# Regrouping modulation steps, moving key transposes in the emitted order, and moving small latent-attention operations between engines, in a two-layer trunk on one core

## The chip, the cores and the metric

The kernel runs on one core of one Trainium2 chip. The metric is the time of one launch in device microseconds (us). The engines are called PE (TensorE, matmuls and transposes), PEld (its loads of stationary operands), DVE (VectorE), ACT (ScalarE), POOL (GpSimd) and SP (SyncE, which issues the DMAs here). Each engine works through its own queue in order and waits at an instruction until the semaphores say that its inputs and its output buffer are ready.

## The reference, cut to what matters

One inference step of a trunk with two layers. 128 prompt tokens and 1024 latent tokens of width 1024 run through each. Layer 0 holds grouped-query attention with rotary keys and a pooling mixer; layer 1 holds a neighbourhood attention (C) and a multi-head latent attention (D) over 128 cached, 1024 latent and 128 prompt keys. Both layers are modulated by shift, scale and gate rows that come from a matmul of the conditioning vector with `w_mod`.

```python
def adaln(cond, w, b):                       # w: 1024 x 3072, cond: the latent request and the prompt
    m = (silu(cond) @ w + b)[:, None, :]
    return split_last(m, (D_MODEL, D_MODEL, D_MODEL))     # shift, scale, gate
def pre_norm(x, g, mod):
    return rms_norm(x, g) * (1 + mod[1]) + mod[0]
def post_residual(x, y, g, mod):
    return x + mod[2] * rms_norm(y, g)
# layer 0, mixer A
q, k, v, ga, ub, gb = split_last(h @ w_in, EVEN_IN_SIZES)  # 512, 128, 128, 512, 512, 512
q, k = axial_rope(rms_norm(q, q_norm)), axial_rope(rms_norm(k, k_norm))
o_a = softmax(q k^T) v ; y = concat(o_a * silu(ga), o_b * silu(gb)) @ w_out
# layer 1, mixer D (8 heads, 64 + 32 columns each)
qd = (rms_norm(cq, q_norm) @ w_uq)                         # w_uq: 384 x 768
kv = (ckv_all @ w_ukv)                                     # w_ukv: 256 x 1024
k_d = concat(kv[..., :64], kpe_all for every head)
o_d = softmax(q_d k_d^T) v_d
```

Everything is float32.

## The kernel before, in words

**Arithmetic.** A float32 product is made of three matmuls in the type fp32r: high times high, high times low and low times high part (`mm3`). So each operand is split into two parts: the high part is a cast, the low part a subtraction. The helpers that record an operation have one line each, and by these lines the profile names them: L97 a matmul, L106 a transpose on TensorE, L109 a DMA on SP's queue, L113 `acopy` (a copy or cast on ScalarE), L118 `vcopy` (the same on VectorE), L121 `vtt` (two tensors on VectorE), L124 `ptt` (two tensors on POOL), L131 `vts` (tensor and scalar on VectorE). L947 is the reduction of the row maxima on VectorE, L952 prepares the maxima for a matmul, L979 is the exponential, L1976 the fill value in `kstep`.

**Order.** No scheduler orders the work: it is emitted by hand, engine by engine in that order. Two functions do the mixing. `weave(main, fill, frac)` (L31) emits a main list of (cost, step) pairs and puts the steps of a fill list between them in proportion to their costs; a step `None` in a fill list emits nothing and only takes up cost. `merge(a, b, off)` (L46) emits the first `off` steps of one fill list and then mixes in another.

**Buffers.** Two pools of slabs hold most operands: "s" (25 buffers) and "w" (17 buffers). PSUM has two tags, A with three banks and B with five (`kn.B` and `kn.C` both take from B). A bank or slab is handed out in the order of the program; the first instruction that writes to it waits for the last one that used it before.

**Stages** (times of the profiled execution): key and value projection of layer 0 to about 70 us; its q stage 70 to 142; gates and the pooling mixer to about 320; the attention units of layer 0 to about 545; the output projection; projections and neighbourhood attention of layer 1 from about 656 to 1090; the token phase of the latent attention to about 1165; its units to about 1500; the last output projection to the end.

**Modulation.** Rows are made by matmuls whose stationary operand is 32 columns wide (`self.sil(k)`, the tile silrep) and which fill one of four 32-row groups of a PSUM bank each. `mod_ss(l)` makes the shift and scale rows: per step k of eight, four matmuls of 512 columns, with two weight slabs wm loaded one step ahead. `mod_gate(l)` makes the gate rows: per k, four matmuls of 256 columns with one slab wg. The layer-1 shift and scale rows are fill steps of the q stage, the gate rows of layer 0 fill steps of items 8 and 9 of the gate stage (on "w" slabs), those of layer 1 fill steps of the first attention unit of layer 0 (on "s" slabs).

**The q stage.** `q_main(0)` and `q_main(1)` are the two halves (256 columns of q each). Each half fills five banks "qkv" with two token tiles each (the fifth holds one), and after each bank `q_evac` norms, scales and rotates the queries (VectorE and ScalarE, rotary partly on POOL). The fill steps of the first half are the keys: `kv1` (norm), `kv2` (rotary on POOL), `kv3` (transposes kT on TensorE, then the casts KH on ScalarE and the subtractions KL on VectorE), and `wl.need(1)`, the split of the second weight chunk.

**The latent attention.** `load_uk`/`split_uk` and `load_uq`/`split_uq` load and split the weights of the next pair of heads (two units); `kstep` makes the keys of a column range in the tile dK, and for the prompt keys (column 1152) in a small tile dKQ, which also takes the rotary key part kpp and a row of ones. The row maxima run ahead of the exponentials: pieces of score matmuls mp are reduced on VectorE (L947), their prepared negatives ms are turned by matmuls mT into a row that is added in the score matmuls st; the exponentials P feed pv, and on POOL the sums acc.

## Time and profile before

| | |
|---|---|
| median of three runs | 1620.8 us (1619.03, 1620.8, 1624.38) |
| profiled execution, its own time | 1616.9 us |
| its span | 1615.1 us |
| mean granted TensorE clock | 0.975 |
| TensorE matmuls busy | 1532.7 us (95%) |
| stationary loads | 1244.7 us (77%) |
| VectorE | 814.4 us (50%) |
| ScalarE | 646.7 us (40%) |
| POOL | 612.7 us (38%) |
| DMA | 104.81 MB, 65 GB/s on the mean |

A profiled row is read like this: start in us, length, engine, line, operation, output and inputs by their tile names, then the shape, the number of instructions, and in brackets the wait ahead of it in us with the instruction that ended it. A row of waits gives the waiting and the releasing instruction, and then the waits' sum, their number and the longest. A row of stretches gives start and end, length, the busy time of PE, PEld, DVE, ACT and POOL with the number of instructions, the granted clock (1.00 is full speed), the busy share of the DMA engines and GB/s.

### The profile page before, as it was taken

How to read it: one execution, taken by the hardware profiler on the slowest of the kernel's cores; microseconds unless marked ns; L12 is line 12 of the kernel's file. 1: busy time of each engine (PE TensorE's matmuls, PEld its weight loads, DVE VectorE, ACT ScalarE, POOL GpSimd, SP SyncE). 2: the span in 40 equal slices, each digit the busy share in tenths (PEclk: the TensorE clock that was granted, in tenths of full speed). 3: DMA queues.
4: the chain of work that ended last, by engine and by line, in shares of the span. 5: the costliest groups of instructions: out<-in, count | busy, mean ns of one | idle time of the engine just before them, and what ended most of it. 6: DMA issues, size and time to landing. Idle time of an engine off the chain costs nothing.

```text
span 1615.1 us, 23601 instructions
## 1 busy us (share of the span) xinstructions
PE 1532.7 (95%) x9095; PEld 1244.7 (77%) x9095; DVE 814.4 (50%) x1796; ACT 646.7 (40%) x1371; POOL 612.7 (38%) x487
## 2 busy tenths in 40 slices
PE   7989999989899999899999999999999899999998
PEld 5978998945555588898989898999966566565786
DVE  4565232347575645534344444424665665645633
ACT  5332211255555333444444544443444343444311
POOL 2643212058669324541303113001156554556421
PEclk8999999999999999999999999999999999999999
DMA  9253004120001122410504131040000000013341
GB/s 345 85 199 86 27 27 150 53 86 14 1 14 40 65 105 79 94 30 15 97 16 82 30 75 38 21 145 11 11 8 20 15 26 15 20 41 104 108 145 52
DMA packets 114080, 104.81 MB, mean 65 GB/s; under 512 B 41776, under 2 KB 99952, under 8 KB 113968
## 3 DMA queue, kind: packets, MB, share of 16 engines
q1 hardware_dynamic: 113792, 103.23, 21.4%
q8 instruction: 72, 1.18, 0.3%
q14 instruction: 40, 0.33, 0.1%
q10 hardware_dynamic: 176, 0.07, 0.0%
HBM read 87.54 MB, written 15.75 MB: 64 GB/s over the span
## 4 chain that ended last, share of the span: by engine, by line
PE 79%; DVE 10%; ACT 5%; issue 3%; POOL 2%; DMA 1%; DVEq 0%; ACTq 0%; SPq 0%; POOLq 0%
PE cg L97 15%; PE yps L97 11%; PE st L97 8%; PE gate L97 8%; PE pv L97 8%; PE lat L97 4%; PE mp L97 4%; PE cpv L97 3%; PE cS L97 2%; PE cT L106 2%; PE dq L97 2%; DVE mx L947 2%; PE qkv L97 2%; PE kv L97 1%; PE modps L97 1%
## 5 line engine op out<-in xcount | busy, mean ns | idle before, releaser
L947 DVE TENSOR_REDUCE mx<-mp 128x1 f32<-128x384 f32 x384 | 189.9, 547 | 108.7 <-PE mp L97 107.3
L124 POOL TENSOR_TENSOR acc<-acc,P 128x1024 f32<-128x1024 f32 x84 | 201.1, 2394 | 86.3 <-ACT P L979 82.5
L979 ACT ACTIVATE P<-st 128x512 f32<-128x512 f32 x256 | 148.1, 598 | 159.1 <-PE st L97 149.3
L124 POOL TENSOR_TENSOR wlo<-raw,whi 128x1024 fp32r<-128x1024 f32 x36 | 87.3, 2427 | 266.9 <-ACT whi L113 205.3
L97 PE MATMUL yps<-whi,ohl 128*128 128x512 f32 x576 | 182.9, 393 | 0.4 <-POOL ohl L124 0.4
L97 PE MATMUL cg<-hT1h,whi 128*128 128x384 f32 x480 | 170.3, 355 | 1.9 <-DVE hf L133 1.2
L97 PE MATMUL cg<-hT1h,wlo 128*128 128x384 f32 x480 | 163.1, 340 | 1.9 <-POOL wlo L124 1.9
L97 PE MATMUL cg<-hT1l,whi 128*128 128x384 f32 x480 | 162.5, 339 | 0.0
L97 PEld LDWEIGHTS yps<-whi,ohl 128*128 128x128 f32 x576 | 108.1, 188 | 25.2 <-issue 2.4
L97 PE MATMUL yps<-wlo,ohl 128*128 128x512 f32 x288 | 112.2, 389 | 0.0
L97 PE MATMUL gate<-hTh,whi 128*128 128x384 f32 x288 | 99.9, 347 | 2.6 <-ACT whi L113 2.6
L97 PE MATMUL gate<-hTh,wlo 128*128 128x384 f32 x288 | 98.9, 344 | 1.6 <-DVE wlo L121 1.6
L97 PE MATMUL gate<-hTl,whi 128*128 128x384 f32 x288 | 98.6, 342 | 0.0
L97 PEld LDWEIGHTS cg<-hT1h,whi 128*128 128x128 f32 x480 | 91.3, 190 | 6.6 <-issue 3.3
L97 PEld LDWEIGHTS cg<-hT1h,wlo 128*128 128x128 f32 x480 | 90.9, 189 | 2.2 <-POOL wlo L124 2.2
L97 PEld LDWEIGHTS cg<-hT1l,whi 128*128 128x128 f32 x480 | 91.3, 190 | 0.6
L1546 ACT ACTIVATE cs<-cs,cnm 128x640 f32<-128x640 f32 (+1 forms) x64 | 54.8, 857 | 91.6 <-DVE cnm L131 90.7
L97 PE MATMUL pv<-P,dV 128*64 128x512 f32 x288 | 77.0, 665 | 0.2
L124 POOL TENSOR_TENSOR acc<-P 128x1024 f32<-128x1024 f32 x14 | 33.5, 2391 | 101.5 <-ACT P L979 100.9
L113 ACT CAST whi<-raw 128x1024 fp32r<-128x1024 f32 (+2 forms) x60 | 61.9, 1037 | 24.6 <-DMA raw<-in_w_in_e 11.5
L97 PE MATMUL st<-QP,KH 128*128 128x512 f32 x144 | 62.7, 435 | 7.6 <-ACT P L979 4.8
L97 PE MATMUL mp<-KH,QP 128*128 128x384 f32 x192 | 57.8, 362 | 6.7 <-DVE msp L1155 2.2
(417 smaller groups left out, 3577.3 us busy)
## 6 DMA issues: line engine op xcount, KB each, us to landing
raw<-in_w_in_o SPq DMA_DIRECT2D x20, 512.0 KB, 4.2
raw<-in_w_in_e SPq DMA_DIRECT2D x18, 512.0 KB, 7.6
wmb<-in_w_mod SPq DMA_DIRECT2D x16, 512.0 KB, 8.2
wm<-in_w_mod SPq DMA_DIRECT2D x16, 512.0 KB, 4.9
wg<-in_w_mod SPq DMA_DIRECT2D x16, 512.0 KB, 4.2
x<-xr SPq DMA_DIRECT2D x9, 512.0 KB, 2.8
xr<-x SPq DMA_DIRECT2D x9, 512.0 KB, 4.7
xn<-in_x_sample SPq DMA_DIRECT2D x8, 512.0 KB, 7.0
```

The lines of the kernel that those rows point to most:

```text
L97: self.nc.tensor.matmul(out=out, lhsT=l, rhs=r, start=st, stop=sp)
L106: self.nc.tensor.transpose(out, in_, self.ident[0:n, 0:n])
L113: self.nc.scalar.copy(out=out, in_=in_)
L124: self.nc.gpsimd.tensor_tensor(out=out, in0=a, in1=b, op=op)
L947: kn.nc.vector.tensor_reduce(out=self.mx[:, h, t, c:c + 1], in_=b, axis=AX.X, op=ALU.max)
L979: kn.nc.scalar.activation(out=P[:, h], in_=a, func=AF.Exp, scale=self.scale)
L1546: nc.scalar.activation(out=s[:, 0:n], in_=s[:, 0:n], func=AF.Exp, bias=nm, accum_out=sm)
```

## The change

Six edits:

- `mod_ss` makes two k in one step (four steps instead of eight) and loads two k ahead.
- `mod_gate` makes `nb` k in one step: two for layer 0, four for layer 1.
- In the fill list of the first q half the empty step of 2000 stands ahead of `wl.need(1)` and the key transposes instead of at the end, the three `kv3` have empty steps between them, and the modulation steps are mixed in from the ninth fill step on instead of the sixth. The gate rows of layer 0 are divided at the middle of their list.
- `split_uk` and `split_uq` make the low part on POOL instead of VectorE.
- `kstep` writes the row of ones on POOL and copies the rotary part on ScalarE; both were on VectorE.
- The first attention unit of layer 0 takes the gate rows of layer 1 with `nb` of 4.

```diff
@@ -232,13 +232,14 @@
         I = self.I
         box = {}
 
-        def step(k):
-            if k == 0:
+        def step(k0):
+            if k0 == 0:
                 box["ps"] = self.C("modps")
             ps = box["ps"]
-            wt = box.pop(k)
-            for j in range(4):
-                self.mm(ps[32 * j:32 * j + 32, :], self.sil(k), wt[j // 2][:, 512 * (j % 2):512 * (j % 2) + 512], k == 0, k == 7)
+            for k in (k0, k0 + 1):
+                wt = box.pop(k)
+                for j in range(4):
+                    self.mm(ps[32 * j:32 * j + 32, :], self.sil(k), wt[j // 2][:, 512 * (j % 2):512 * (j % 2) + 512], k == 0, k == 7)
 
         def load(k):
             wt = [self.W([128, 1024], name="wm") for _ in range(2)]
@@ -263,14 +264,14 @@
                 self.vtt(d[l].rearrange("p (j i) s -> p i j s", j=2), v[:, :, j:j + 2, 0:2], bc, ALU.add)
             self.vtt(self.sc[l], self.sc[l], self.gpre[:, l, :, None].to_broadcast([128, 8, 2]))
 
-        L = [(1, lambda: load(0))]
-        for k in range(8):
-            if k < 7:
-                L.append((1, lambda k=k: load(k + 1)))
-            L.append((1000, lambda k=k: step(k)))
+        L = [(1, lambda: load(0)), (1, lambda: load(1))]
+        for k in range(0, 8, 2):
+            L += [(1, lambda k=k: load(k)) for k in (k + 2, k + 3) if k < 8]
+            L.append((2000, lambda k=k: step(k)))
         return L + [(1, fin), (600, fin2)]
 
-    def mod_gate(self, l, al=None):
+    def mod_gate(self, l, al=None, nb=2):
+
         I = self.I
         al = al or self.W
         box = {}
@@ -279,12 +280,13 @@
             box[k] = al([128, 1024], name="wg")
             self.dma(box[k], I["w_mod"][l, 128 * k:128 * k + 128, 2048:3072])
 
-        def step(k):
-            if k == 0:
+        def step(k0):
+            if k0 == 0:
                 box["ps"] = self.C("modg")
-            wt = box.pop(k)
-            for j in range(4):
-                self.mm(box["ps"][32 * j:32 * j + 32, 0:256], self.sil(k), wt[:, 256 * j:256 * j + 256], k == 0, k == 7)
+            for k in range(k0, k0 + nb):
+                wt = box.pop(k)
+                for j in range(4):
+                    self.mm(box["ps"][32 * j:32 * j + 32, 0:256], self.sil(k), wt[:, 256 * j:256 * j + 256], k == 0, k == 7)
 
         def fin():
             bm = al([128, 2, 256], name="bg")
@@ -293,11 +295,10 @@
             self.vtt(self.ggrow[l], box["ps"][:, 0:256], bm[:, 0], ALU.add)
             self.vtt(self.ggrow[l], self.ggrow[l], bm[:, 1])
 
-        L = [(1, lambda: load(0))]
-        for k in range(8):
-            if k < 7:
-                L.append((1, lambda k=k: load(k + 1)))
-            L.append((500, lambda k=k: step(k)))
+        L = [(1, lambda k=k: load(k)) for k in range(nb)]
+        for k in range(0, 8, nb):
+            L += [(1, lambda k=k: load(k)) for k in range(k + nb, min(8, k + 2 * nb))]
+            L.append((500 * nb, lambda k=k: step(k)))
         return L + [(1, fin)]
 
     def gg(self, l, s):
@@ -782,11 +783,11 @@
     gs = Stream([Chunk(kn, w_in[:, c:c + 128], 128, veng=True) for _, _, c in gl])
 
     fill = [(1, lambda: kv1(0)), (500, lambda: kv1(2)), (500, lambda: kv1(1)), (800, lambda: kv2(0)), (800, lambda: kv2(2)),
-            (800, lambda: kv2(1)), (500, lambda: wl.need(1)), (500, lambda: kv3(0)), (500, lambda: kv3(2)),
-            (500, lambda: None), (500, lambda: kv3(1)), (2000, lambda: None)]
+            (800, lambda: kv2(1)), (2000, lambda: None), (500, lambda: wl.need(1)), (500, lambda: kv3(0)),
+            (500, lambda: None), (500, lambda: kv3(2)), (500, lambda: None), (500, lambda: kv3(1)), (500, lambda: None)]
     mods = kn.mod_ss(1)
     q_alloc(0)
-    weave(q_main(0), merge(fill, mods[:2], 6), 1.0)
+    weave(q_main(0), merge(fill, mods[:2], 9), 1.0)
     q_alloc(1)
     fill = mods[2:]
     fill = fill[:4] + [(1, lambda: gs._load(0))] + fill[4:]
@@ -910,7 +911,7 @@
             if kind == "gb":
                 fill = pool_mixer(g, *pool, dd) + fill
         if i in (8, 9):
-            a, b = (0, 8) if i == 8 else (8, nm)
+            a, b = (0, nm // 2) if i == 8 else (nm // 2, nm)
             fill += mods0[a:b]
         if i == 10:
             fill += units[0].prep(kn.W)
@@ -1288,7 +1289,7 @@
         xn[t] = y
 
     pre, run = outproj(kn, 0, xin, put, lambda t, x: kn.dma(x1[128 * t:128 * t + 128, :], x))
-    tail = run_units(kn, units, side, extra={0: kn.mod_gate(1, kn.S), 7: [(18000, lambda: None)] + pre})
+    tail = run_units(kn, units, side, extra={0: kn.mod_gate(1, kn.S, 4), 7: [(18000, lambda: None)] + pre})
     pg = lambda g, ks: [(350, lambda g=g, k=k: H.make(g, k, xn[3 * g:3 * g + 3])) for k in ks]
     mix = lambda ks: [a for k in ks for g in range(2) for a in pg(g, (k,))]
     w_in = I["w_in_o"][0]
@@ -1945,7 +1946,7 @@
         r2v = r2.rearrange("p k t h d -> p (k t h d)")
         hv = hl.rearrange("p s k t c -> p s (k t c)")
         kn.acopy(hv[:, 0], r2v)
-        kn.vtt(hv[:, 1], r2v, f32(hv[:, 0]), ALU.subtract)
+        kn.ptt(hv[:, 1], r2v, f32(hv[:, 0]), ALU.subtract)
         self.w["k", p] = hl
 
     def split_uq(self, p, al=None):
@@ -1960,7 +1961,7 @@
         h_ = al([128, 3, 2, 128], F32R, name="uqh")
         l_ = al([128, 3, 2, 128], F32R, name="uql")
         kn.acopy(h_, r)
-        kn.vtt(l_, r, f32(h_), ALU.subtract)
+        kn.ptt(l_, r, f32(h_), ALU.subtract)
         self.w["q", p] = (h_, l_)
 
     def kstep(self, p, c0, n):
@@ -1973,9 +1974,9 @@
         if c0 >= 1152:
             self.KQ = kn.W([97, 4, 2, 128], F32R, name="dKQ")
             self.Kp = self.KQ[:, 0:2]
-            kn.nc.vector.memset(f32(self.Kp[96:97]), 1.0)
+            kn.nc.gpsimd.memset(f32(self.Kp[96:97]), 1.0)
             for h in range(2):
-                kn.vcopy(self.Kp[64:96, :, h, :], f32(self.kpp[64:96]))
+                kn.acopy(self.Kp[64:96, :, h, :], f32(self.kpp[64:96]))
             hi = [self.Kp[:, 0, h, :] for h in range(2)]
             lo = [self.Kp[:, 1, h, :] for h in range(2)]
         else:
```

## The prediction

> **What bounds the kernel now.** I read the page first (busy shares, clock), then TensorE's waits, then the timeline of every engine around each wait that the change touches.

> ```profile
> PE 1532.7 (95%) x9095; PEld 1244.7 (77%) x9095; DVE 814.4 (50%) x1796; ACT 646.7 (40%) x1371; POOL 612.7 (38%) x487
> PE mT L97 <- DVE ms L952: 6.5, 3, 2.2
> PE kT L106 <- POOL k L124: 4.6, 2, 2.4
> ```

> TensorE is busy 95% of the span, so work elsewhere counts only where TensorE stands still or where the array is badly filled. The two waits below the busy line (us in total, times, longest), with one of 2.60 us further down, are the ones that the change aims at. They cost more than their length, because the granted clock halves behind some of them. Columns below: the stretch, its length, busy time of five engines, then the clock, the share of DMA and GB/s.

> ```profile
> 92.25:95.76 3.51, 3.51 (x19) 3.51 (x18) 2.93 (x10) 2.11 (x4) 1.97 (x2) 0.52 0.94 315
> 95.76:105.96 10.20, 8.10 (x67) 7.69 (x66) 6.61 (x12) 4.41 (x14) 3.86 (x3) 1.00 0.75 264
> 419.60:423.40 3.80, 3.69 (x19) 2.29 (x20) 3.80 (x8) 1.23 (x3) 2.65 (x2) 0.56 0.00 0
> 1191.50:1198.50 7.00, 7.00 (x27) 6.42 (x27) 5.03 (x11) 3.85 (x5) 2.65 (x1) 0.51 0.00 0
> 1256.81:1261.40 4.59, 4.59 (x20) 1.77 (x20) 2.02 (x1) 1.05 (x2) 1.47 (x1) 0.68 0.02 4
> ```

> **Modulation rows in pairs and fours.** One visit of a modulation step to the array, against the matmuls around it:

> ```profile
> 112.50 0.28 PE L97 MATMUL qkv<-whi,hTl 128*128 128x256 f32 x1
> 112.71 1.06 PE L97 MATMUL modps<-wm,silrep 128*32 128x512 f32 x8
> 113.93 0.28 PE L97 MATMUL qkv<-wlo,hTh 128*128 128x256 f32 x1
> ...
> 266.33 0.34 PE L97 MATMUL gate<-hTh,wlo 128*128 128x384 f32 x1
> 266.59 0.64 PE L97 MATMUL modg<-wg,silrep 128*32 128x256 f32 x8
> 267.45 0.34 PE L97 MATMUL gate<-hTl,whi 128*128 128x384 f32 x1
> ...
> 54.74 1.95 PE L97 MATMUL modps<-wmb,silrep 128*32 128x128 f32 x64
> ```

> From 112.50 to 113.93 pass 1.43 us; two q-stage matmuls would take 0.24 of it (8.10 busy us for 67 in the stretch from 95.76, 0.12 each), so the visit costs 1.19. By the same count a gate-row visit costs 267.45 - 266.33 - 2 x 0.17 = 0.78 (1532.7 us for 9095 instructions, 0.17 each). Columns 512 and 256 differ by 0.41, so the columns take 0.82 and 0.41, and some 0.35 us is paid for each visit whatever it holds. The row at 54.74 holds eight k of 128 columns in one visit: 1.95 us, against 8 x 0.21 = 1.7 for the columns, so further k in a visit add their columns and next to nothing more. Visits go from 8 to 4 in the q stage, 8 to 4 in the gate stage (`mod_gate(0)`), 8 to 2 in the first attention unit (`mod_gate(1)`): 4 x 0.35 = **1.4**, **1.4** and 6 x 0.35 = 2.1, taken as **2.0** us of TensorE time, and TensorE sets the pace at all three.

> The same transfers are made, two or four k ahead instead of one (KB each, us to landing):

> ```profile
> wm<-in_w_mod SPq DMA_DIRECT2D x16, 512.0 KB, 4.9
> ```

> In the gate stage I count 16 of the 17 "w" buffers held at the worst point, in the first unit 23 of 25 "s" buffers. In the q stage the second buffer of load 3 stands on SP until the first q chunk is read out, no later than the second q half starts (105.96, where the second stretch above ends), and loads 4 and 5 queue behind it. 106 + 4.9 = 111, and by the order of the list the second pair is wanted after 113: the matmuls between hide it, and I cost it at nothing; without that cover it would cost up to 4.9 once. In the first unit the two fours now come after 17 and 19 of the 25 row-maxima pieces instead of among them, so VectorE's reductions follow each other without those gaps; that may give back up to 2.0, or gain up to 1.5 because the gate rows are finished earlier: 2.0 stands, ends 0 and 3.5.

> **Key transposes later.** The first transpose that waits now (the second has the other 2.2 of the 4.6 us), and what surrounds it:

> ```profile
> 86.27 0.66 PE L106 MATMUL kT<-ident,k 128*128 128x128 f32 x4 [2.39 <-POOL k L124]
> 102.49 0.39 PE L97 MATMUL qkv<-whi,hTh 128*128 128x256 f32 x1 [1.74 <-ACT KH L113]
> ...
> 94.29 0.69 DVE L121 TENSOR_TENSOR q<-qkv,hr 128x512 f32<-128x512 f32 x1
> 97.03 2.89 DVE L121 TENSOR_TENSOR wlo<-raw,whi 128x1024 fp32r<-128x1024 f32 x2
> 99.85 1.38 DVE L121 TENSOR_TENSOR KL<-kT,KH 64x512 fp32r<-64x512 f32 x2
> 101.26 1.17 ACT L113 CAST KH<-kT 64x512 fp32r<-64x512 f32 x2 [4.35 <-DVE KL L121]
> 108.71 2.00 DVE L121 TENSOR_TENSOR t<-q,rtq 128x128 f32<-128x128 f32 x4
> ```

> The list of emitted steps puts the first transpose from the 38th to the 51st k of the first q half: TensorE is there at about 88.1, after its operand. Both POOL waits (4.6 us) and the half clock behind them (3.5 us at 0.52, 1.7 lost) go. What is late next is PSUM: five "B" banks, handed out in order of release (the wait at 102.49, on ScalarE's KH, fits that). TensorE reaches the last q tile at about 93.6 with all five taken. The first is released by the VectorE product at 94.29 (end 95.0), the next only after VectorE's weight subtraction (99.92) and then the square's reduction (0.69, as the product of as many elements), ScalarE's root and the reciprocal (0.7 together, an estimate from the same row), and the product 0.69: 102.0. The third key transpose waits for that from 96.1. The bank after it belongs to the first transpose: rotary 2.0 (104.1), KL 1.38, KH 1.17, so 106.7. The second q half starts at about 106.7; now at 105.96. So the waits change places: -0.8 for the start, about -0.3 for a bank that the first pair waits for, and -0.6 for a one-in-three risk that the half clock reaches past 106.7 (1.7). With the four visits saved (+1.4) the q stage gives **-0.3**; ends -2 and, if the banks come free as now, +7.

> **VectorE relieved in the latent attention.** First the row of the prompt keys (`kstep` at column 1152), in the first unit and at the end of three later ones:

> ```profile
> 1190.06 0.41 PE L97 MATMUL mp<-dKh,QH 96*128 96x384 f32 x1 [2.60 <-DVE dKQ L121]
> 1186.88 2.42 DVE L118 CAST dKQ<-kpp 32x256 fp32r<-32x256 f32 x2
> 1189.32 0.59 DVE L121 TENSOR_TENSOR dKQ<-dk,dKQ 64x128 fp32r<-64x128 f32 x2
> ...
> 1256.81 1.01 PE L97 MATMUL mT<-negid,ms 128*1 128x128 f32 x8 [2.17 <-DVE ms L952]
> 1253.22 0.53 ACT L113 CAST dKQ<-dk 64x128 fp32r<-64x128 f32 x2
> 1253.20 0.48 DVE L1976 MEMSET dKQ<- 1x512 f32 x1 [0.16 <-issue]
> L113 ACT CAST Rhl<-srow x17: 404/407/408, 372.4 to 1511.0; 128x256 fp32r<-128x256 f32 x17
> ```

> The fill value and the two casts hold VectorE 0.48 + 2.4 us ahead of the subtraction that releases the bank. On ScalarE no trace shows them; the nearest row, an SBUF cast of 256 elements, is 0.41, so 0.81 ahead of the casts of 0.53. In the first unit that ends before TensorE is ready at 1187.46: 2.6 saved, and the 7.0 us at clock 0.51 behind it (3.4 lost) lose their cause. The 6.0 become **5.5**, since VectorE's reductions come denser then; ends 2 and 6. At the unit ends: 1253.22 + 0.81 + 0.53 + 0.59 + 0.3 for the last reduction = 1255.4 instead of 1256.81, 1.4 saved and 0.7 of wait left, too short for a half clock by any row here; the half clock behind it (4.59 x 0.32 = 1.5) goes. 3 x 2.9 = 8.7, taken as **8.0**, as the exponentials behind the copies start 0.8 later; ends 4 and 8.8. POOL's fill value (0.5 at VectorE's rate) is wanted only four steps later.

> The weight subtractions: `split_uk` is wanted ten or more us later and hidden by that, and that of the token phase likewise. `split_uq` at the end of units 0, 2 and 4 is not:

> ```profile
> 1220.25 0.39 PE L97 MATMUL dq<-hT1h,uql 128*128 128x512 f32 x1
> 1308.42 0.50 PE L97 MATMUL dq<-hT1h,uql 128*128 128x512 f32 x1 [0.37 <-DVE uql L121]
> 1215.20 5.48 POOL L124 TENSOR_TENSOR acc<-acc,P 128x1024 f32<-128x1024 f32 x2 [1.31 <-ACT P L979]
> 1302.72 4.83 POOL L124 TENSOR_TENSOR acc<-acc,P 128x1024 f32<-128x1024 f32 x2 [3.75 <-ACT P L979]
> L124 POOL TENSOR_TENSOR t<-q,rtq 128x512 f32<-128x512 f32 x8 | 10.3, 1288 | 22.6 <-DVE q L121 22.6
> 419.19 0.45 PE L97 MATMUL mp<-KH,QP 128*128 128x384 f32 x1 [1.64 <-DVE mx L947]
> ```

> On POOL it stands behind the last two additions of the unit. POOL takes 1.29 for 512 elements and 2.4 for 1024, so 1.84 for 768. Unit 0: additions done at 1220.0 (4.8 without VectorE beside them), product 1221.9, wanted at 1220.25: 1.6 lost. Unit 2: 1307.55 + 1.84 = 1309.4 plus 0.1 against 1308.42: 1.1, and unit 4 like it: 3.8 us, 1.4 to 1.6 of wait in one piece each time. Of two waits of that size quoted here the one at 419.19 (1.64) was followed by clock 0.56, the one at 102.49 (1.74) by 1.00. So half the chance of 1.7 each: 2.5. **-6.3**; ends -3.8 and -8.9.

> [...]

> **Sum.** 1.4 + 2.0 - 0.3 + 5.5 + 8.0 - 6.3 = 10.3 us. It is made against the profiled execution, 1616.9 us with a span of 1615.1: 1606.6. The three timed runs have median 1620.8; less 10.3 that is **1610.5**. About 0.3% (4.9 us) is what a measurement of this kernel can tell from no change.

> **Rivals.**
> *Stalls vanish in the q stage*: if a bank is free at 96 and 104, the stage gains 7 instead of -0.3: 1603. For it: the waits in the list are on POOL. Against: five banks and VectorE's order. Chance 0.08.
> *No half clock behind the new waits on POOL*: the term is -3.8 and the time 1608.0. For it: 102.49. Against: 419.19. [...] Chance 0.17.
> *Relief half returned*: reductions and ScalarE take up half of the latent gains (2.7 and 4), every new wait halves the clock (-8.9), the fours give 1, the q stage -2: -1.8 with the gate rows, 1622.6. For it: the waits at 1190.06 and 1256.81 both end on VectorE, and what a relief frees, the next reduction in line may take. Chance 0.20.
> *Slower*: ScalarE's copies wait for the fill value, which now stands in POOL's queue behind an addition of 2.4. Two additions stand there at each unit's end; from 1253.2 with one of 2.4 and the fill value of 0.5 the copies would start at about 1256.2 and the reduction end 1.6 later than now, three times, and in the first unit 1.5 later: -6.3 in place of +13.5, and the time 1630.3. It decides as soon as a write to another partition range of the tile counts as a conflict. Against: ScalarE's cast at 1253.22 began 0.46 us before VectorE's fill value (from 1253.20) was done. Chance 0.07.

> **Numbers.** The forecast has 0.48. Faster 0.48 + 0.08 + 0.17 = 0.73, same 0.20, slower 0.07. Low: 1604, most of the q-stage rival; high 1622, near the relief half returned; outside lie 0.05 and 0.12. The likeliest case alone: 1606 to 1615.

> **What would show it.** Right: 4, 4 and 2 visits, the pairs about 2.0 and the fours about 1.9 us; kT without waits on POOL, but a wait of some 6 us on VectorE before the third kT; mp on dKQ gone; mT on ms at 0.7; dq on POOL uql at about 1.5. Wrong: mT still at 2 us, a dq wait above 3, or a q stage that ends well away from the present 141.9.

## The result, and the profile after

| | median | runs | lowest to highest |
|---|---|---|---|
| before | 1621.45 us | 4 | 1619.03 to 1624.38 |
| changed | 1602.98 us | 4 | 1600.49 to 1606.68 |

The ratio is 0.9887, 95% interval [0.9868, 0.9906]: 18.5 us less, by the interval 15 to 21. The forecast was 10.3 us less, and 1602.98 lies 1 us below its range. The profiled execution of the changed kernel took 1600.49 us with a span of 1598.7; between the two profiles lie 16.4 us. The working by stages below is made on those 16.4.

From the page of the changed kernel, and from its list of TensorE's waits (us in total, times, longest):

```profile
PE 1518.5 (95%) x9095; PEld 1238.9 (77%) x9095; DVE 793.5 (50%) x1776; ACT 649.4 (41%) x1379; POOL 625.0 (39%) x499
PE kT L106 <- DVE q L121: 5.6, 1, 5.6
PE dq L97 <- POOL uql L124: 4.4, 3, 1.5
PE mT L97 <- DVE ms L953: 2.0, 3, 0.7
```

TensorE's busy time fell by 14.2 us with the same 9095 matmuls, its waits only by the other 2. So most of the gain is matmuls that ran at full instead of half clock, or without the price of a visit. The half-clock stretches held 76.1 us of TensorE's work in the profile before and 52.2 in the one after. Just ahead of 95.76 us in the profile before, at granted clock 0.50, the matmuls qkv of 128x256 start 0.21 us apart, and just behind it, at 1.00, 0.12; so half of the difference, 11.9 us, is a rough estimate of what the clock gave. The waits of kT on POOL and of mp on dKQ are gone, mT's fell from 6.5 to 2.0, and two new ones stand where the prediction put them.

The time line of the changed kernel, at the places of the prediction's rows:

```profile
1181.72 0.71 ACT L113 CAST dKQ<-kpp 32x256 fp32r<-32x256 f32 x2
1182.44 0.54 ACT L113 CAST dKQ<-dk 64x128 fp32r<-64x128 f32 x2
1185.91 0.52 POOL L1977 MEMSET dKQ<- 1x512 f32 x1
...
1212.58 0.50 PE L97 MATMUL dq<-hT1h,uql 128*128 128x512 f32 x1 [1.51 <-POOL uql L124]
1247.71 0.64 PE L97 MATMUL mT<-negid,ms 128*1 128x128 f32 x8 [0.66 <-DVE ms L953]
...
103.64 1.08 PE L106 MATMUL kT<-ident,k 128*128 128x128 f32 x4 [5.65 <-DVE q L121]
108.16 0.58 PE L97 MATMUL qkv<-whi,hTh 128*128 128x256 f32 x1 [0.24 <-ACT KH L113]
```

ScalarE's two copies take 0.71 us, and its casts follow them 3.5 us ahead of POOL's fill value: they do not wait for it. At the three unit ends the copies start 2.6 us ahead of that fill value. dq waits 1.51 us, mT 0.66.

To place the gain I took the start of the same matmul in both profiles. The table gives by how much the changed kernel (first profile, and a second one of the run after_again below) moved against the kernel before between two such points; negative is earlier.

| stretch of the kernel before (us) | what lies there | first | second |
|---|---|---|---|
| 0 to 34 | nothing of the change | +1.6 | +0.6 |
| 34 to 139 | q stage, key transposes, four visits | -0.6 | -0.6 |
| 139 to 262 | nothing of the change | -2.1 | -1.9 |
| 262 to 300 | gate rows of layer 0 | -0.9 | -0.9 |
| 300 to 358 | first attention unit, two fours | -2.6 | -2.4 |
| 358 to 1187 | nothing of the change | +1.4 | +0.8 |
| 1187 to 1198 | prompt keys of the first latent unit | -6.2 | -6.2 |
| 1198 to 1221, 1262 to 1309, 1350 to 1397 | uql on POOL | +1.8, +1.0, +0.8 | +1.8, +1.0, +0.8 |
| 1221 to 1262, 1309 to 1350, 1397 to 1439 | prompt keys at three unit ends | -2.9, -3.1, -3.1 | -2.9, -3.1, -3.1 |
| 1439 to 1468 | nothing of the change | -1.6 | -1.6 |

The rows of the change add up to -15.8 in the first profile. The four others (+1.6, -2.1, +1.4, -1.6) lie where the change does nothing. I take them for DMA times at the start and for half-clock stretches that fell or did not fall behind waits that both kernels have; no run separates these two.

### The profile page after: what moved, and what is told of

It is laid out like the page before. It is cut to its first block, busy times and chain, and to the rows that moved or that the text cites. A ratio compares the mean times of both kernels' runs of the same rounds, so it can differ in the third digit from the quotient of the medians.

```text
span 1598.7 us, 23592 instructions
## 1 busy us (share of the span) xinstructions
PE 1518.5 (95%) x9095; PEld 1238.9 (77%) x9095; DVE 793.5 (50%) x1776; ACT 649.4 (41%) x1379; POOL 625.0 (39%) x499
## 5 line engine op out<-in xcount | busy, mean ns | idle before, releaser
L124 POOL TENSOR_TENSOR acc<-acc,P 128x1024 f32<-128x1024 f32 x84 | 199.7, 2378 | 75.0 <-ACT P L980 70.0
L124 POOL TENSOR_TENSOR wlo<-raw,whi 128x1024 fp32r<-128x1024 f32 x36 | 87.5, 2433 | 266.5 <-ACT whi L113 153.2
L97 PE MATMUL yps<-whi,ohl 128*128 128x512 f32 x576 | 182.8, 393 | 0.3 <-POOL ohl L124 0.3
L97 PE MATMUL cg<-hT1h,whi 128*128 128x384 f32 x480 | 170.3, 355 | 1.9 <-DVE hf L133 1.2
L97 PE MATMUL cg<-hT1h,wlo 128*128 128x384 f32 x480 | 163.4, 341 | 1.9 <-POOL wlo L124 1.9
L97 PE MATMUL cg<-hT1l,whi 128*128 128x384 f32 x480 | 162.9, 339 | 0.0
L97 PEld LDWEIGHTS yps<-whi,ohl 128*128 128x128 f32 x576 | 108.1, 188 | 25.2 <-issue 2.4
L97 PE MATMUL yps<-wlo,ohl 128*128 128x512 f32 x288 | 112.2, 389 | 0.0
L97 PE MATMUL gate<-hTh,whi 128*128 128x384 f32 x288 | 98.1, 341 | 4.2 <-ACT whi L113 4.2
L97 PE MATMUL gate<-hTh,wlo 128*128 128x384 f32 x288 | 97.8, 340 | 1.3 <-DVE wlo L121 1.3
L97 PE MATMUL gate<-hTl,whi 128*128 128x384 f32 x288 | 97.5, 339 | 0.0
L97 PEld LDWEIGHTS cg<-hT1h,whi 128*128 128x128 f32 x480 | 91.3, 190 | 6.6 <-issue 3.3
L97 PEld LDWEIGHTS cg<-hT1h,wlo 128*128 128x128 f32 x480 | 91.2, 190 | 2.2 <-POOL wlo L124 2.2
L97 PEld LDWEIGHTS cg<-hT1l,whi 128*128 128x128 f32 x480 | 91.4, 190 | 0.4
L124 POOL TENSOR_TENSOR acc<-P 128x1024 f32<-128x1024 f32 x14 | 33.6, 2398 | 102.3 <-ACT P L980 101.7
L113 ACT CAST whi<-raw 128x1024 fp32r<-128x1024 f32 (+2 forms) x60 | 61.9, 1037 | 24.1 <-DMA raw<-in_w_in_e 11.0
L97 PE MATMUL pv<-P,dV 128*64 128x512 f32 x288 | 71.4, 622 | 0.2
L97 PE MATMUL st<-QP,KH 128*128 128x512 f32 x144 | 61.8, 429 | 6.6 <-ACT P L980 3.8
L97 PE MATMUL mp<-KH,QP 128*128 128x384 f32 x192 | 57.3, 357 | 6.8 <-DVE msp L1156 2.2
## 6 DMA issues: line engine op xcount, KB each, us to landing
raw<-in_w_in_o SPq DMA_DIRECT2D x20, 512.0 KB, 4.0
raw<-in_w_in_e SPq DMA_DIRECT2D x18, 512.0 KB, 7.2
wmb<-in_w_mod SPq DMA_DIRECT2D x16, 512.0 KB, 8.4
wm<-in_w_mod SPq DMA_DIRECT2D x16, 512.0 KB, 6.5
wg<-in_w_mod SPq DMA_DIRECT2D x16, 512.0 KB, 4.6
x<-xr SPq DMA_DIRECT2D x9, 512.0 KB, 2.8
xr<-x SPq DMA_DIRECT2D x9, 512.0 KB, 4.8
xn<-in_x_sample SPq DMA_DIRECT2D x8, 512.0 KB, 7.1
```

Source lines behind the costliest of these rows:

```text
L97: self.nc.tensor.matmul(out=out, lhsT=l, rhs=r, start=st, stop=sp)
L113: self.nc.scalar.copy(out=out, in_=in_)
L124: self.nc.gpsimd.tensor_tensor(out=out, in0=a, in1=b, op=op)
```

## The experiments

Each line gives the median, the ratio to the kernel before and its 95% interval. The kernel before had medians of 1619.3 to 1619.7 us in these comparisons.

| run | us | ratio | interval |
|---|---|---|---|
| only_mods | 1615.61 | 0.9975 | 0.9955 to 0.9995 |
| only_order | 1619.74 | 0.9996 | 0.9974 to 1.0019 |
| only_latent | 1605.77 | 0.9919 | 0.9895 to 0.9942 |
| after_again | 1601.39 | 0.9892 | 0.9864 to 0.9919 |
| uq_late | 1608.32 | 0.9942 | 0.9919 to 0.9964 |
| uq_early | 1600.28 | 0.9893 | 0.9870 to 0.9915 |
| wl_pool | 1600.51 | 0.9897 | 0.9869 to 0.9925 |
| both | 1598.66 | 0.9882 | 0.9859 to 0.9905 |
| uq_back | 1599.51 | 0.9872 | 0.9848 to 0.9896 |
| kstep_vec | 1601.60 | 0.9886 | 0.9865 to 0.9908 |
| best2 | 1596.47 | 0.9860 | 0.9839 to 0.9881 |
| swap | 1603.98 | 0.9899 | 0.9881 to 0.9918 |

### The parts by themselves, and the whole again

**only_mods**: the diff's hunks of `mod_ss`, `mod_gate` and their callers, nothing else.

> The kernel before with the modulation steps in pairs and fours alone (layer-1 shift and scale rows, gate rows of both layers). Theory A (a fixed price of some 0.35 us for each visit of 32-column tiles): 14 visits fewer give 4.8 us, about 1.4 in the q stage, 1.4 between 256 and 292 us, 2.0 to 2.7 in the first attention unit; ratio 0.997. Theory B (the visits cost only their columns and the gain seen between 292 and 356 us of the changed kernel was a half-clock window that happened not to fall there): under 1.5 us in all, ratio 0.999 to 1.000.

Measured 4.1 us less (interval 1 to 7). The first unit gave 2.5 us between 300 and 358 us. Visits of the changed kernel:

```profile
111.52 0.28 PE L97 MATMUL qkv<-whi,hTl 128*128 128x256 f32 x1
111.74 1.92 PE L97 MATMUL modps<-wm,silrep 128*32 128x512 f32 x16
113.59 0.38 PE L97 MATMUL qkv<-whi,hTh 128*128 128x256 f32 x1
...
329.67 0.39 PE L97 MATMUL st<-QM,KL 65*128 65x512 f32 x1
330.00 1.93 PE L97 MATMUL modg<-wg,silrep 128*32 128x256 f32 x32
331.86 0.50 PE L97 MATMUL st<-QP,KH 128*128 128x512 f32 x1
```

A pair takes 113.59 - 111.52 = 2.07 us from neighbour to neighbour, where two single visits take 1.43 each. By the time alone theory B (at most 1.5 us) isn't out of the interval, so the traces have to decide. In after_again (below) the half clock came behind the same two waits as in the kernel before, in stretches from 323.2 and 347.1 us as against 324.5 and 351.8, and 300 to 358 us was still 2.4 us shorter. So the gain there is no half-clock stretch that happened not to fall, and theory A stands. But 1.0 us of it is a wait of st on the exponentials, which fell from 3.95 to 2.93 us and may come of the new order. The price of a visit shows in the rows above: without the 0.24 us of the two neighbours a pair takes 1.83 us and two visits 2.38, so a visit spared is worth 0.55 here, where the prediction had 0.35; in the gate stage it was worth 0.2 (0.9 us for four). So it isn't one price for all places.

**only_order**: the fill list and the offset 9.

```diff
-    fill = [..., (800, lambda: kv2(1)), (500, lambda: wl.need(1)), (500, lambda: kv3(0)), ..., (2000, lambda: None)]
+    fill = [..., (800, lambda: kv2(1)), (2000, lambda: None), (500, lambda: wl.need(1)), (500, lambda: kv3(0)), ...]
```

> The kernel before with the later key transposes alone (fill list of the first q half and the mixing offset). Theory A (the waits only change places, to a PSUM bank behind VectorE's chain): the waits of kT on POOL (4.6 us) and of the first matmul behind it (1.7) go, one of 5 to 6 us on VectorE's q comes, with up to three half-clock windows of which most is idle; the q stage ends within 2 us of the kernel before, ratio 0.998 to 1.001. Theory B (the stage gains in earnest): it ends 3 us or more earlier, ratio 0.997 or lower.

No change in time that can be told. Its TensorE time line shows the exchange of waits, with 5.66 us in place of the 5.65 of the whole change:

```profile
96.02 0.38 PE L97 MATMUL qkv<-whi,hTh 128*128 128x256 f32 x1 [1.36 <-DVE q L121]
103.01 1.08 PE L106 MATMUL kT<-ident,k 128*128 128x128 f32 x4 [5.66 <-DVE q L121]
```

**only_latent**: `split_uk`, `split_uq` and `kstep` as changed.

> The kernel before with the moves off VectorE in the latent attention alone (both weight subtractions and the fill value to POOL, the copies of the rotary part to ScalarE). Theory A (by the two traces, stage by stage): 6 us at the first unit, three times 3 at the unit ends, less three times 1.0 to 1.6 at the products on uql, without half clock behind these: 11 to 13 us, ratio 0.992 to 0.993. Theory B (as the prediction had it, half the new waits of 1.5 us halve the clock): 7 us, ratio 0.9955.

13.9 us less, theory A. The three parts add up to 4.1 + 0.0 + 13.9 = 18.0 us, the whole gave 18.3 in the same comparison. No interaction can be told, though each of these differences is known only to 3 or 4 us.

**after_again**: the changed kernel unaltered.

> The changed kernel itself once more, for a second profile and a tighter time. Theory A (the granted clock is set for fixed stretches of 3.41 us that run through the program, by the idle share of the stretch before, and where these stretches lie differs from execution to execution): the same waits come back at the same places within 0.3 us, but the half-clock stretches behind waits of 1.7 to 2.7 us are not all the same ones as in the first profile, none stands behind the three waits of 1.5 us on uql, and each begins a whole number of 3.413 us after the others. Theory B (a wait of more than about 1.35 us halves the clock by itself, by what runs then): the same waits have the same half-clock stretches as in the first profile. Time by both: ratio 0.987 to 0.991.

Theory A. One wait that both profiles have, of cS on VectorE's maxima (2.04 us in each), was followed by full clock in the first and by half clock in the second. First profile, then second; the stretches are of 3.413 us, as in the clock's own records in the traces, and start where these put them (columns as in the prediction: the stretch, its length, busy time of PE and the other engines, clock, DMA share, GB/s):

```profile
809.13:812.54 3.41, 1.70 (x10) 1.67 (x11) 2.44 (x11) 1.55 (x5) 0.58 (x2) 1.00 0.02 5
812.54:815.96 3.42, 3.42 (x33) 3.19 (x33) 2.43 (x10) 3.03 (x9) 0.00 (x0) 1.00 0.00 0
```

```profile
807.85:811.26 3.41, 1.37 (x9) 1.19 (x8) 2.56 (x11) 1.03 (x4) 0.71 (x3) 1.00 0.00 0
811.26:814.67 3.41, 3.41 (x14) 3.23 (x13) 2.01 (x9) 2.53 (x6) 0.00 (x0) 0.50 0.02 5
```

In the first the wait was cut by the border of a stretch (1.71 us idle in the one, the rest in the one before); in the second it lay whole in one, with 2.04 idle. Only the second halved the clock. Behind the waits of 1.5 us on uql neither profile has a half-clock stretch; nor have the profiles of only_latent, wl_pool and kstep_vec, which have the same waits, so that it is none behind 15 of them. Twelve of them left 1.4 to 1.5 us idle in one stretch, and three were cut by a border.

### The size of a wait against the clock

**uq_late**: a fill of the target ahead of the subtraction (it is written over at once).

```diff
+        kn.nc.gpsimd.memset(f32(l_), 0.0)
         kn.ptt(l_, r, f32(h_), ALU.subtract)
```

> The changed kernel with one more POOL instruction (a fill of the 128x768 target) ahead of each subtraction of split_uq, so that the three waits of 1.5 us on uql grow. The fill isn't in any trace; by the reduction of the fill values seen (1x1152 in 1.0 us) some 0.7 us: waits of about 2.2. Theory A (the granted clock halves for the next of the fixed 3.41-us stretches when TensorE idled 1.7 us or more of one, wherever the stretches happen to lie): at 2.2 us the half clock follows behind two of three, on average 0.6 each, where it followed behind none at 1.5: 2.1 us of wait and 3 us of clock, about 5 us longer than the changed kernel, ratio to before 0.9923. Theory B (half the chance for any wait above 1.35, whatever its length): 2.1 us of wait and no more half clocks than at 1.5, ratio 0.9905.

6.9 us longer than after_again, theory A. The fill took 0.74 us, the waits became 2.31, 2.25 and 2.23, and the half clock followed behind two of the three. The first, of 2.31 us, was cut by a border into 0.78 and 1.53 us of idle, and full clock followed. The stretches around the other two:

```profile
1298.68 0.73 PE L97 MATMUL dq<-hT1h,uql 128*128 128x512 f32 x1 [2.25 <-POOL uql L124]
1295.36:1298.77 3.41, 1.16 (x6) 0.64 (x5) 0.00 (x0) 0.89 (x2) 3.19 (x3) 1.00 0.00 0
1298.77:1302.19 3.42, 3.42 (x8) 2.65 (x9) 0.00 (x0) 0.18 (x1) 0.00 (x0) 0.50 0.51 153
1384.11:1387.52 3.41, 1.18 (x6) 0.65 (x6) 0.00 (x0) 0.87 (x2) 3.15 (x3) 1.00 0.00 0
1387.52:1390.94 3.42, 3.42 (x9) 2.64 (x10) 0.00 (x0) 0.24 (x1) 0.00 (x0) 0.50 0.44 153
```

So 0.75 us more of POOL work, three times, cost more than twice what it is long: three times by the medians, 2.4 times (5.5 us) by the starts of matmuls at these waits and in the stretches behind them. Theory B, the one the prediction used, would have given no more half clocks than at 1.5 us.

**uq_early**: `(2 * p, 8)` becomes `(2 * p, 7)` for `split_uq`. **uq_back**: `kn.ptt` becomes `kn.vtt` again in `split_uq` alone.

> The changed kernel with split_uq one key step earlier in units 0, 2 and 4, so that POOL's subtraction stands ahead of the last two additions. Theory A (the new waits on uql cost their length alone): 4.4 us of waits go, nothing else; 4 us shorter than the changed kernel, ratio 0.9867. Theory B (they cost half-clock stretches as well, as the prediction put it): 6 us or more. Theory C (the additions and with them the end of the unit are now late instead): the time stays.

> The changed kernel with the subtraction of split_uq on VectorE again, all else as changed. Theory A (on POOL it costs the length of three waits of 1.5 us, and no clock): the waits on uql fall from 4.4 us to about 1, 3 to 3.5 us shorter than the changed kernel, ratio to before 0.987. Theory B (as the prediction had it, 3.8 us of wait and 2.5 of clock): 6 us shorter, ratio 0.9855. Theory C (VectorE, loaded again, is late with something else): the time stays.

By its time uq_early is theory C: it can't be told from after_again, and its interval ends at 0.9870, just above theory A's 0.9867. Its waits on uql are gone, but the exponentials now stand behind ScalarE's cast of uqh, and the first row below came instead (the changed kernel has one such wait, of 0.5 us); its profile also has half clock of 6.8 us from 1446.5, which the two of the changed kernel have not. uq_back has the two others:

```profile
PE st L97 <- ACT QH L113: 2.1, 3, 0.8
```

```profile
PE mT L97 <- DVE ms L953: 2.0, 3, 0.7
PE dq L97 <- DVE uql L121: 1.0, 2, 0.5
```

uq_back is 1.9 us shorter than after_again and 3.5 shorter than the changed kernel's first median. Its interval holds the ratios of all three theories, so the time doesn't choose between them. The starts of matmuls speak for theory A: from 1198 to 1221 and from 1350 to 1397 uq_back stands still where the changed kernel lost 1.8 and 0.8. From 1262 to 1309 it lost 1.4 all the same, beside half clock of 6.8 us behind a wait of 2.1 us on dKl, which the changed kernel has too. VectorE, with the subtraction to do again, lets mT wait no longer, which is against theory C.

### What in `kstep` it was

**kstep_vec**: the copies on VectorE again, the fill value left on POOL.

```diff
-                kn.acopy(self.Kp[64:96, :, h, :], f32(self.kpp[64:96]))
+                kn.vcopy(self.Kp[64:96, :, h, :], f32(self.kpp[64:96]))
```

> The changed kernel with the two copies of the rotary part on VectorE again; the fill value stays on POOL. Theory A (the copies are what held VectorE ahead of the subtraction, and a wait of 1.7 us or more halves the clock where the fixed stretches let it): a wait of about 2.1 us on dKQ comes back in the first unit and the three waits on ms grow from 0.7 to 1.7 to 2.1; 5 to 6 us of waits and 3 to 4 of clock, 9 us longer than the changed kernel, ratio to before 0.995. Theory B (the fill value was the larger part): under 4 us longer, ratio 0.991 to 0.992.

Both theories missed. It lost nothing at all against the changed kernel: the wait on dKQ is 0.2 us, and mT is no longer in the list of TensorE's waits. The row of the copies (shortest, median and longest in ns) shows why, in the kernel before and then in kstep_vec:

```profile
L118 DVE CAST dKQ<-kpp x8: 276/1214/2218, 1186.9 to 1432.7; 32x256 fp32r<-32x256 f32 x8
```

```profile
L118 DVE CAST dKQ<-kpp x8: 273/282/402, 1180.3 to 1414.9; 32x256 fp32r<-32x256 f32 x8
```

The same copy on the same engine takes 0.28 us in the one and up to 2.2 in the other. The time line of the kernel before has the partner:

```profile
1253.34 4.94 POOL L124 TENSOR_TENSOR acc<-acc,P 128x1024 f32<-128x1024 f32 x2 [1.01 <-ACT P L979]
1253.70 2.37 DVE L118 CAST dKQ<-kpp 32x256 fp32r<-32x256 f32 x2
```

The row of POOL holds two additions, and the first of them runs from 1253.34 to 1255.71. The copies come 0.36 us after its start; the first ends at 1255.86, the second, of 0.28 us, at 1256.07. It is the same at all four places: the long copy ends 0.15 us after POOL's addition. So I formed a new theory: they are held up by POOL's addition, and the fill value ahead of them is what made them late. **swap** tries it on the kernel before, with every instruction on its old engine:

```diff
-            kn.nc.vector.memset(f32(self.Kp[96:97]), 1.0)
             for h in range(2):
                 kn.vcopy(self.Kp[64:96, :, h, :], f32(self.kpp[64:96]))
+            kn.nc.vector.memset(f32(self.Kp[96:97]), 1.0)
```

> The kernel before with one edit: VectorE makes the two copies of the rotary part first and writes the fill value behind them; nothing changes its engine. Theory A (the copies are 0.3 us each and stood 2.4 us in the kernel before because POOL's addition had begun 0.3 us ahead of them and held them up until it ended; 0.48 us earlier they are ahead of it): two copies in 0.5 to 0.6 us, the wait of 2.6 us in the first unit falls to about 0.6, the three of 2.15 on ms to about 0.8; with the half clocks behind them 13 to 16 us shorter than the kernel before, ratio 0.990 to 0.992. Theory B (VectorE needs the time for the copies and the fill value in any order): two copies in 2.4 us, the waits as before, ratio 0.999 to 1.001.

Theory A, in the waits as well. Time line of swap:

```profile
1249.81 0.49 DVE L118 CAST dKQ<-kpp 32x256 fp32r<-32x256 f32 x2
1250.08 5.38 POOL L124 TENSOR_TENSOR acc<-acc,P 128x1024 f32<-128x1024 f32 x2 [1.00 <-ACT P L979]
1250.44 0.48 DVE L1978 MEMSET dKQ<- 1x512 f32 x1
1251.67 0.64 PE L97 MATMUL mT<-negid,ms 128*1 128x128 f32 x8 [0.29 <-DVE ms L952]
```

The copies start 0.27 us ahead of the addition and take 0.49 together; mT waits 0.29 instead of 2.17. Moving one line below another, on the same engine, gives a ratio of 0.9899, which can't be told from that of all six edits together. The ratio is helped by the missing cost of uql on POOL.

### Versions that go further

**wl_pool**: the low part of the second q chunk on POOL, made before the keys.

```diff
+    wl.need(1)
     fill = [(1, lambda: kv1(0)), ...
-            ..., (2000, lambda: None), (500, lambda: wl.need(1)), ...
+            ..., (2000, lambda: None), (500, lambda: None), ...
```

with `veng=True` taken from that chunk. **both** is wl_pool and uq_early, **best2** is wl_pool and uq_back.

> The changed kernel with the weight split of the second q chunk emitted ahead of the keys and its subtraction on POOL, so that VectorE's 2.9 us no longer stand between the products that release the PSUM banks. Theory A (the wait of 5.6 us before the third key transpose is VectorE's chain on the banks): the wait falls by about 2.9 us and the three half-clock stretches around it become one or two; 3 to 5 us shorter than the changed kernel, ratio 0.987. Theory B (another link of the chain takes its place: POOL, which now has 4.9 us more to do ahead of the rotary products, or ScalarE): within 1 us of the changed kernel.

> The changed kernel with both edits: split_uq one key step earlier and the second q chunk's subtraction on POOL ahead of the keys. If both hold, 7 to 9 us shorter than the changed kernel, ratio to before 0.984; if only the first holds, 0.9867.

> The changed kernel with split_uq on VectorE again and the second q chunk's subtraction on POOL ahead of the keys. If both gains add: 3 us and 2 to 3 us shorter than the changed kernel, ratio to before 0.985 to 0.986. If neither can be told from no change by the time: 0.988 to 0.990.

```profile
99.79 1.09 PE L106 MATMUL kT<-ident,k 128*128 128x128 f32 x4 [2.85 <-DVE q L121]
```

In wl_pool the wait before the third key transpose fell from 5.65 to 2.85 us, by the length of the subtraction taken away, and in best2, which has the same edit, the stretch from 83 to 139 us is 3.4 us shorter than in the kernel before, against 0.5 in the changed kernel. That bears out the chain on the banks. The times of wl_pool and both can't be told from the changed kernel's: wl_pool has the wait of theory A with the time of theory B, and both, expected at 0.984 or 0.9867, came out above either, with the second inside its interval. best2 has the lowest median of all that ran, 1596.47 us, some 5 us below after_again, and its ratio is the one expected if both gains add; but its interval [0.9839, 0.9881] overlaps that of after_again. swap was not tried on top of it.

## Why the prediction was wrong, by its own steps

The direction, the places and the waits were right; the size was not. The step that failed is the price of uql on POOL, the term of -6.3 us: it held 2.5 us for half clocks behind the new waits, and none came. Beside it, all but one of the gains were taken too small. Against the table above:

| term | predicted gain | measured |
|---|---|---|
| q stage with four visits | -0.3 | 0.6 |
| gate rows in pairs | 1.4 | 0.9 |
| gate rows in fours | 2.0 | 2.6 |
| prompt keys, first unit | 5.5 | 6.2 |
| prompt keys, unit ends | 8.0 | 9.1 |
| uql on POOL | -6.3 | -3.6 |
| sum | 10.3 | 15.8 |

**uql on POOL.** This term makes 2.7 of the 5.5 us between the two sums. The waits came out as worked out: 1.51, 1.45 and 1.44 us, 3.5 more than before against 3.8 predicted. The 2.5 us on top, "half the chance of 1.7 each", did not come. That chance was taken from two waits, 1.64 with and 1.74 without half clock, as if the length of a wait left it to luck. What counted is how much of one fixed stretch was idle. Over the 14 profiles of this case, of the stretches at full clock in which TensorE idled 1.9 us or more, all 148 were followed by half clock; at 1.65 to 1.9 us, 51 of 63; at 0.9 to 1.65, 25 of 154; below that, 1 of 5875. In the profiles before and after alone it was 22 of 22, 9 of 12, 5 of 21 and 0 of 838. The 15 waits of 1.5 us on uql left at most 1.5 us idle in one stretch, and none halved the clock; of the three of 2.23 to 2.31 us in uq_late, two lay whole in a stretch and did, and the one that a border cut did not. That was the rival "no half clock behind the new waits": it happened, and uq_late shows the other side.

**Prompt keys.** The sizes were nearly right and the reason was not, which is luck: the change took the copies off VectorE whole, whatever made them long. The prediction read 2.42 us as what two copies cost VectorE. They cost 0.56; the rest was waiting for POOL, which the row hid inside the busy time. Taking them to ScalarE, taking the fill value away, or swapping the two each ends it: the three unit ends together became 9.1, 11.4 and 10.1 us shorter, the first unit 6.2, 5.6 and 3.4 (the profile of swap still has a half-clock stretch there, from 1191.2). The prediction worked out 6.0 and 8.7 here and took 5.5 and 8.0; 6.2 and 9.1 came.

**q stage.** Right in mechanism: the third key transpose was forecast to be released at 102.0 and to wait from 96.1; it waited 5.65 us and was released at 103.64 in a profile that ran 1.6 us later from the start. The visits carry the stage: from 34 to 139 us the profile of only_order is 1.4 us longer than the kernel before, that of only_mods 1.7 us shorter.

**The range.** Three terms were shaded downward and one given a penalty by chance. These leanings, all to the same side, add up: with 6.0, 8.7 and -3.8 the sum is 14.0 us, and 1606.8. The lower end then was set by one rival alone, not by the good ends of the terms together, and so lay above the result. The terms don't explain all of the miss: 1620.8 less the measured 15.8 us would be 1605.0, still above 1602.98. The medians lie 18.5 us apart and the profiles 16.4, and executions of the kernel before differ by 15 us (below), so the last 2 us stay open. The rivals "stalls vanish", "relief half returned" and "slower" did not come: only_order gave nothing, VectorE's reductions took nothing back, and ScalarE's copies start 2.6 us or more ahead of POOL's fill value.

## What to carry to other kernels

Look at the shortest and the longest of one instruction before you price its removal: the copy that took 0.28 us at best and 2.2 at worst was waiting inside its busy time, and a change of order (swap, ratio 0.9899) did what the change of engines in only_latent did (0.9919). Price a stall of TensorE by what it leaves idle in one clock stretch: 1.5 us cost 1.5 here; 2.25 us, where half clock followed, cost some 1.7 more, an estimate from the 3.42 us of work at 0.50 behind it. And sum the ends of the terms for the range, rather than lean on each in the same direction.

## What the runs showed of the hardware

**VectorE beside POOL.** Where the copy dKQ<-kpp on VectorE started 0.29 to 0.36 us after an addition on POOL, it ended 0.15 us after that addition (2.15 to 2.22 us at four places of the kernel before, instead of 0.28); where it started 0.27 us ahead of the addition it was not held up (1249.81 in swap, 0.49 for two). What in the chip makes the copy wait, the rows don't show.
